# A gate-and-up projection with four K pairs as seven block products instead of three, and sums made by a DMA that adds

## The chip, the cores and the metric

The kernel runs on one core of one Trainium2 chip. The metric is the device time of one execution in microseconds (us). The profile was taken from one more execution, which has its own time.

## The reference

Two encoder layers over 256 tokens of 2048 features, all in float32. Each layer has a mixer (windowed attention, a convolution group and a gating group behind one input projection `w_in`, joined by `w_out`) and then a SwiGLU block, which is what the change touches:

```python
def swiglu(h, w_gate, w_up, w_down):
    return (jax.nn.silu(h @ w_gate) * (h @ w_up)) @ w_down

h = rms_norm(x, ffn_norm_g[l])
x = x + swiglu(h, w_gate[l], w_up[l], w_down[l])
```

`h` is 256 x 2048, `w_gate` and `w_up` are 2048 x 5632, `w_down` is 5632 x 2048.

## The kernel before

**Float32 from three products.** TensorE (PE) multiplies in a shortened format. So each weight tile is split into a high part `wh` (a cast on ScalarE, ACT, L136) and a low part `wl` (the rest, a subtraction on VectorE, DVE, L137), each activation tile likewise, and every product is three matmuls (`three_tok`, L410 to L412): high by high, low by high, high by low.

**Weights.** The host packs all weights into chunks of 128 x 2048, in the order of use. `Weights.load` brings a chunk into one of three `raw` buffers, by a DMA on SyncE's queue (SP, L94). `Weights.split` cuts it into units of at most 1024 columns and fills one of five pairs of `wh` and `wl` buffers. When the last unit of a chunk is split, the next chunk is asked for. `take` runs the splitting four units ahead of PE.

**Gate and up.** `gate_up` makes 512 columns of gate and of up for all 256 tokens. It is called 22 times, 11 for each layer. K is 2048, 16 tiles of 128, taken as eight pairs in the order of `UP_PAIRS`. The two token tiles and the two halves (gate, up) of a pair's weights make a 2 x 2 by 2 x 2 block product. A pair of kind "P" does it with eight products in two units. A pair of kind "S" does it in the Winograd way, with seven products in four units: two that come straight from the raw chunk (1024 and 512 columns) and two that are sums of weights. The first sum `f` has 1024 columns, one DVE addition (L101); the second, `g`, two DVE additions of 512 columns from `f` and raw columns. The sums of activations are made once for a layer (`feed_sums`). `f` and `g` lie in tiles with the tags `hm6` and `hm7`, which the mixer uses before.

**Results.** The products run into seven PSUM banks, m1 to m7. After the last S pair of a call (`LAST_S`) banks 1, 6 and 7 are read (L472 to L474), after the last pair the others (L476 to L480). Then silu and the multiplication (L828, L829). The tile is transposed during the next call (`hidden_parts`). After two or three calls a down projection follows (`ad` tiles).

**What sets the order.** A scheduler with a model of its own orders the instructions of each engine when the kernel is built; the tile pools give a buffer to a new tile when the last reader of the old one is done. Each engine and each DMA queue works its list in order.

The lines that matter: `UP_PAIRS` (L50), `Weights.load` (L87), `source` (L103), `split` (L125), `sum_tile` (L194), `gate_up` (L418).

Of the kernel before, what the change touches and what calls it, by code (L numbers as in the profile page):

```python
# [10 lines left out]
F32 = mybir.dt.float32  # L11
F32R = mybir.dt.float32r
AF = mybir.ActivationFunctionType
ALU = mybir.AluOpType
# [3 lines left out]
P = 128  # L18
D = 2048
S = 256  # L20
# [5 lines left out]
TAPS = 31  # L26
HALO = TAPS // 2
EPS = 1e-6
NU = 16
NEG = -3.0e38  # L30
SCALE = 1.0 / math.sqrt(128.0)
CH = 2048
HC = CH // 2
# [13 lines left out]
             (0, MIX_CONV, 1, 1, 1), (1, MIX_CONV, 1, 1, 1)]  # L47


UP_PAIRS = [(4, "P"), (5, "S"), (6, "P"), (7, "S"), (0, "P"), (1, "S"), (2, "P"), (3, "P")]  # L50
KIND = dict(UP_PAIRS)
LAST_S = max(i for i, (_, kind) in enumerate(UP_PAIRS) if kind == "S")

# [11 lines left out]
class Weights:  # L65
# [8 lines left out]
    def __init__(self, nc, w, kinds, raw_pool, split_pool, sum_tile):  # L74
        self.nc, self.w = nc, w
        self.n = w.shape[0]
        assert len(kinds) == self.n
        self.raw_pool, self.split_pool, self.sum_tile = raw_pool, split_pool, sum_tile
        self.units = [
            (i, u) for i in range(self.n) for u in range(4 if kinds[i] == "S" else 2)  # L80
        ]
        self.kinds = kinds
        self.raw, self.sums, self.parts = {}, {}, {}
        self.loaded = self.split_done = 0
        self.cur, self.off, self.width = -1, 0, 0

    def load(self, pieces=1, after_first=None):  # L87
        i = self.loaded
        if i >= self.n:
            return  # L90
        t = self.raw_pool.tile([P, CH], F32, tag="raw", name=f"raw{i}")
        for k in range(pieces):
            c = slice(k * CH // pieces, (k + 1) * CH // pieces)
            self.nc.sync.dma_start(t[:, c], self.w[i, :, c])  # L94
            if k == 0 and after_first:
                after_first()
        self.raw[i] = t
        self.loaded += 1

    def add(self, out, a, b):  # L100
# [2 lines left out]
    def source(self, i, u):  # L103
        raw = self.raw[i]
        if self.kinds[i] != "S":
            return raw[:, u * HC:(u + 1) * HC]
        if u == 0:
            return raw[:, HC:]
        if u == 1:
            return raw[:, 512:HC]  # L110
        if u == 2:
            f = self.sum_tile(0)
            self.add(
                f.rearrange("p (a b) -> p a b", a=2),
                raw[:, 0:512].unsqueeze(1).to_broadcast([P, 2, 512]),
                raw[:, 512:512 + HC].rearrange("p (a b) -> p a b", a=2),
            )
            self.sums[i] = f
            return f
        g = self.sum_tile(1)  # L120
        self.add(g[:, :512], self.sums.pop(i)[:, 512:], raw[:, 512:HC])
        self.add(g[:, 512:], g[:, :512], raw[:, HC + 512:])
        return g
# [36 lines left out]
def chunk_kinds():  # L160
    kinds = []
    for _ in range(DEPTH):
        kinds += ["P"] * (MIX_COLS * KT // CH + D * KT // CH)
        for _, gn in PARTS:
            kinds += [kind for _, kind in UP_PAIRS] * gn
            kinds += ["P"] * (4 * gn * D // CH)
# [4 lines left out]
def encoder_kernel(  # L171
# [15 lines left out]
    hpool = ctx.enter_context(tc.tile_pool(name="hpool", bufs=1))  # L187
    units = ctx.enter_context(tc.tile_pool(name="units", bufs=NU))
    tmp = ctx.enter_context(tc.tile_pool(name="tmp", bufs=2))
# [2 lines left out]
    pm = ctx.enter_context(tc.tile_pool(name="pm", bufs=2, space=PSUM))  # L192

    def sum_tile(i):  # L194
        return hpool.tile([P, HC], F32, tag=f"hm{6 + i}", name=f"fs{i}")

    W = Weights(nc, w, chunk_kinds(), raw_pool, split_pool, sum_tile)

    def unit(name, dtype=F32):
# [23 lines left out]
    hm = []  # L223
# [194 lines left out]
    def gate_up(forms, pending):  # L418
# [7 lines left out]
        plan = []  # L426
        for i, kind in UP_PAIRS:
            if kind == "S":
# [27 lines left out]
        for b, block in enumerate(plan):  # L456
            if b == 1 and pending:
                hidden_parts(*pending)
            if UP_PAIRS[b][1] == "S":
                for m, x, _ in block:  # L460
# [33 lines left out]
    def proj(kts, part, g):  # L494

        accs = [ps.tile([P, 512], F32, tag="ps", name=f"acc{i}") for i in range(g)]
        for i, k in enumerate(kts):
            wh, wl = W.take(g * P)
            for j in range(g):
                c = slice(j * P, (j + 1) * P)  # L500
                three(accs[j][:, :S], wh[:, c], wl[:, c], part(k, 0), part(k, 1),
                      i == 0, i == len(kts) - 1)
        return accs
# [205 lines left out]
    for l in range(DEPTH):  # L709
# [22 lines left out]
        for c in range(2, 4):  # L732
            a = proj(range(KT), xs_part, 1)[0]
            g = proj(range(KT), xs_part, 1)[0]
# [17 lines left out]
        for g in range(2):  # L752
            a = proj(range(KT), xs_part, 1)[0]
# [9 lines left out]
        for p in range(4):  # L763
            qT = unit2("qT")
            for hh in range(2):
                a = proj(range(KT), xs_part, 1)[0]
# [49 lines left out]
        def hidden_parts(ht, i0):  # L816
            for i in range(0, 4, 2):
                pt = transposed(ht, i)
                d = hm[(i0 + i) // 2]
                hilo(d[:, :, :S], d[:, :, S:], pt)  # L820

        for g0, gn in PARTS:
# [13 lines left out]
            for n in range(NG):  # L836
                acc = token_acc("ad")
                f = slice(n * G, (n + 1) * G)
# [34 lines left out]
def _pack_weights(w_in, w_out, w_gate, w_up, w_down):  # L873
# [17 lines left out]
    for l in range(DEPTH):  # L891
# [18 lines left out]
        for g0, gn in PARTS:  # L910
            for j in range(g0, g0 + gn):
                c = slice(j * G, (j + 1) * G)
                gu = np.concatenate([w_gate[l][:, c], w_up[l][:, c]], axis=1)
                for i, kind in UP_PAIRS:
                    pair = (2 * i, 2 * i + 1)
# [74 lines left out]
```

## Time and profile before

| | us |
|---|---|
| median of 3 runs (2002.52 to 2003.04) | 2002.74 |
| the profiled execution | 2004.66 |
| its span in the trace | 2002.9 |
| PE busy | 1973.4 |
| DVE busy | 1561.3 |
| ACT busy | 1060.3 |
| POOL (GpSimd) busy | 28.2 |

The span runs from the first to the last instruction. A busy time is the union of an engine's instructions; matmuls overlap one another, so their pace is read from their starts. A name such as `wl<-fs,wh` says that a `wl` tile was written from an `fs` and a `wh` tile. The releaser of a wait is the instruction whose end ended it.

### The profile page before, as it was taken

The numbers are of one execution on the slowest core, as the hardware profiler recorded it, in microseconds if no ns is written. First come the engines' busy times: TensorE is split into PE (matmuls) and PEld (weight loads), VectorE is DVE, ScalarE is ACT, GpSimd is POOL, SyncE is SP. The second block draws the span as 40 slices with busy tenths as digits, with TensorE's granted clock in tenths as the row PEclk, the third lists the DMA queues.
The fourth block names the chain that finished last, engine by engine and source line by source line (L and its number), as shares of the span: only waits on it lengthen the run. The fifth ranks groups of instructions, "written<-read, shape, count | busy, mean of one in ns | idle before, by whom it ended". The sixth has DMA issues, their size and how long they took to land.

```text
span 2002.9 us, 25520 instructions
## 1 busy us (share of the span) xinstructions
PE 1973.4 (99%) x9998; PEld 1683.8 (84%) x9998; DVE 1561.3 (78%) x1986; ACT 1060.3 (53%) x1367; POOL 28.2 (1%) x50
## 2 busy tenths in 40 slices
PE   8999999999999999999999999999999999999998
PEld 8998887888888888888899888788888888888886
DVE  8997679866886688578679975798678857985785
ACT  6356556544554455445544565665445544554553
POOL 3000000000000000000000000000000000000000
PEclk9999999999999999999999999999999999999999
DMA  7554544565555455555545435355545555555553
GB/s 276 202 183 154 203 158 178 198 212 186 192 208 208 170 210 204 196 189 204 196 169 190 148 139 202 143 192 207 210 170 208 211 191 187 210 204 192 192 204 111
DMA packets 55993, 380.96 MB, mean 190 GB/s; under 512 B 6336, under 2 KB 8640, under 8 KB 10560
## 3 DMA queue, kind: packets, MB, share of 16 engines
q1 hardware_dynamic: 55872, 379.33, 52.3%
q8 instruction: 78, 1.28, 0.2%
q14 instruction: 43, 0.35, 0.1%
HBM read 377.21 MB, written 2.10 MB: 189 GB/s over the span
## 4 chain that ended last, share of the span: by engine, by line
PE 97%; ACT 1%; DVE 1%; DMA 0%; issue 0%; SPq 0%; POOLq 0%; DVEq 0%
PE m L410 15%; PE m L411 15%; PE m L412 15%; PE ad L411 8%; PE ad L412 8%; PE ad L410 8%; PE acc L394 4%; PE acc L395 4%; PE acc L396 4%; PE ao L410 3%; PE ao L412 3%; PE ao L411 3%; PE pt L294 1%; PE acct L514 1%; PE acct L515 1%; PE acct L516 1%
## 5 line engine op out<-in xcount | busy, mean ns | idle before, releaser
L136 ACT CAST wh<-raw 128x1024 fp32r<-128x1024 f32 (+1 forms) x706 | 700.4, 1009 | 695.2 <-PE ad L412 243.5
L137 DVE TENSOR_TENSOR wl<-raw,wh 128x1024 fp32r<-128x1024 f32 (+1 forms) x706 | 816.7, 1168 | 313.8 <-ACT wh L136 310.7
L411 PE MATMUL m<-wl,xs 128*128 128x512 f32 x858 | 336.0, 392 | 0.0
L412 PE MATMUL m<-wh,xs 128*128 128x512 f32 x858 | 333.8, 391 | 0.0
L410 PE MATMUL m<-wh,xs 128*128 128x512 f32 x858 | 310.8, 392 | 7.1 <-ACT xg L317 7.1
L411 PE MATMUL ad<-wl,h 128*128 128x512 f32 x704 | 274.5, 390 | 0.0
L410 PE MATMUL ad<-wh,h 128*128 128x512 f32 x704 | 274.3, 391 | 0.0
L412 PE MATMUL ad<-wh,h 128*128 128x512 f32 x704 | 272.1, 390 | 0.0
L136 ACT CAST wh<-fs 128x1024 fp32r<-128x1024 f32 x132 | 138.8, 1053 | 159.8 <-PE m L412 133.8
L394 PE MATMUL acc<-xs,wh 128*128 128x256 f32 x704 | 196.8, 287 | 8.1 <-ACT xs L283 8.1
L395 PE MATMUL acc<-xs,wh 128*128 128x256 f32 x704 | 200.7, 287 | 0.0
L396 PE MATMUL acc<-xs,wl 128*128 128x256 f32 x704 | 200.3, 287 | 0.0
L137 DVE TENSOR_TENSOR wl<-fs,wh 128x1024 fp32r<-128x1024 f32 x132 | 159.9, 1220 | 47.7 <-ACT wh L136 47.5
L410 PEld LDWEIGHTS m<-wh,xs 128*128 128x128 f32 x858 | 162.4, 189 | 40.3 <-ACT xg L317 7.5
L412 PEld LDWEIGHTS m<-wh,xs 128*128 128x128 f32 x858 | 162.3, 189 | 33.9
L411 PEld LDWEIGHTS m<-wl,xs 128*128 128x128 f32 x858 | 162.1, 189 | 33.8
L412 PEld LDWEIGHTS ad<-wh,h 128*128 128x128 f32 x704 | 132.2, 188 | 27.3
L410 PEld LDWEIGHTS ad<-wh,h 128*128 128x128 f32 x704 | 132.2, 188 | 27.1
L411 PEld LDWEIGHTS ad<-wl,h 128*128 128x128 f32 x704 | 132.2, 188 | 26.9
L394 PEld LDWEIGHTS acc<-xs,wh 128*128 128x128 f32 x704 | 134.4, 194 | 8.7 <-ACT xs L283 8.4
L395 PEld LDWEIGHTS acc<-xs,wh 128*128 128x128 f32 x704 | 136.8, 194 | 0.2
L396 PEld LDWEIGHTS acc<-xs,wl 128*128 128x128 f32 x704 | 136.5, 194 | 0.2
(180 smaller groups left out, 2636.0 us busy)
## 6 DMA issues: line engine op xcount, KB each, us to landing
raw<-w SPq DMA_DIRECT2D x349, 1024.0 KB, 4.8
x<-xT SPq DMA_DIRECT2D x16, 128.0 KB, 4.6
raw<-w SPq DMA_DIRECT2D x4, 512.0 KB, 7.0
lr<-lrow SPq DMA_DIRECT2D x2, 1024.0 KB, 4.9
xt<-xN SPq DMA_DIRECT2D x2, 1024.0 KB, 6.0
raw<-w SPq DMA_DIRECT2D x4, 256.0 KB, 4.3
gf<-lrow SPq DMA_DIRECT2D x1, 1024.0 KB, 6.6
out<-xt SPq DMA_DIRECT2D x2, 448.0 KB, 3.5
```

The lines of the kernel that those rows point to most:

```text
L136: self.nc.scalar.copy(out=h[:, c], in_=r[:, c])
L137: self.nc.vector.tensor_tensor(out=lo[:, c], in0=r[:, c], in1=h[:, c].bitcast(F32), op=ALU.subtract)
L294: nc.tensor.transpose(pt[:, i, t * P:(t + 1) * P], src[t][:, (i0 + i) * P:(i0 + i + 1) * P], ident,)
L394: nc.tensor.matmul(acc, wh, xh, start=first, stop=False)
L395: nc.tensor.matmul(acc, wh, xl, start=False, stop=False)
L396: nc.tensor.matmul(acc, wl, xh, start=False, stop=last)
L410: nc.tensor.matmul(a, xh, wh, start=first, stop=False)
L411: nc.tensor.matmul(a, xh, wl, start=False, stop=False)
L412: nc.tensor.matmul(a, xl, wh, start=False, stop=last)
L514: nc.tensor.matmul(a, xh, wh, start=(k == 0), stop=False)
L515: nc.tensor.matmul(a, xh, wl, start=False, stop=False)
L516: nc.tensor.matmul(a, xl, wh, start=False, stop=(k == KT - 1))
```

## The change

`UP_PAIRS` gets a fourth "S" and another order of kinds: P S S P S P S P in place of P S P S P S P P. So a call has 60 products, and its last S pair is the seventh of eight instead of the sixth. The host packs the weights by the same table.

`f` is no longer added on DVE. When a chunk of kind "S" is loaded, `load` also issues a DMA on SP that writes the chunk's first 512 columns twice into a sum tile, and a DMA on GpSimd's queue that adds columns 512 to 1535 to it, straight from the weights in memory. `f` alternates between two tiles, one with a tag of its own (`fs`) and `hm6`; `g` takes `hm7`. The pool of small tiles grows from 16 to 17.

```diff
--- before.py
+++ after.py
@@ -26,7 +26,7 @@
 TAPS = 31
 HALO = TAPS // 2
 EPS = 1e-6
-NU = 16
+NU = 17
 NEG = -3.0e38
 SCALE = 1.0 / math.sqrt(128.0)
 CH = 2048
@@ -47,7 +47,7 @@
              (0, MIX_CONV, 1, 1, 1), (1, MIX_CONV, 1, 1, 1)]
 
 
-UP_PAIRS = [(4, "P"), (5, "S"), (6, "P"), (7, "S"), (0, "P"), (1, "S"), (2, "P"), (3, "P")]
+UP_PAIRS = [(4, "P"), (5, "S"), (6, "S"), (7, "P"), (0, "S"), (1, "P"), (2, "S"), (3, "P")]
 KIND = dict(UP_PAIRS)
 LAST_S = max(i for i, (_, kind) in enumerate(UP_PAIRS) if kind == "S")
 
@@ -81,7 +81,7 @@
         ]
         self.kinds = kinds
         self.raw, self.sums, self.parts = {}, {}, {}
-        self.loaded = self.split_done = 0
+        self.loaded = self.split_done = self.n_sums = 0
         self.cur, self.off, self.width = -1, 0, 0
 
     def load(self, pieces=1, after_first=None):
@@ -95,6 +95,14 @@
             if k == 0 and after_first:
                 after_first()
         self.raw[i] = t
+        if self.kinds[i] == "S":
+
+            f = self.sum_tile(self.n_sums % 2)
+            self.n_sums += 1
+            w12 = self.w[i, :, 0:512].unsqueeze(1).to_broadcast([P, 2, 512])
+            self.nc.sync.dma_start(f.rearrange("p (a b) -> p a b", a=2), w12)
+            self.nc.gpsimd.dma_start(f, self.w[i, :, 512:512 + HC], accum_op=ALU.add)
+            self.sums[i] = f
         self.loaded += 1
 
     def add(self, out, a, b):
@@ -109,15 +117,8 @@
         if u == 1:
             return raw[:, 512:HC]
         if u == 2:
-            f = self.sum_tile(0)
-            self.add(
-                f.rearrange("p (a b) -> p a b", a=2),
-                raw[:, 0:512].unsqueeze(1).to_broadcast([P, 2, 512]),
-                raw[:, 512:512 + HC].rearrange("p (a b) -> p a b", a=2),
-            )
-            self.sums[i] = f
-            return f
-        g = self.sum_tile(1)
+            return self.sums[i]
+        g = self.sum_tile(2)
         self.add(g[:, :512], self.sums.pop(i)[:, 512:], raw[:, 512:HC])
         self.add(g[:, 512:], g[:, :512], raw[:, HC + 512:])
         return g
@@ -192,7 +193,8 @@
     pm = ctx.enter_context(tc.tile_pool(name="pm", bufs=2, space=PSUM))
 
     def sum_tile(i):
-        return hpool.tile([P, HC], F32, tag=f"hm{6 + i}", name=f"fs{i}")
+        tag = ("fs", "hm6", "hm7")[i]
+        return hpool.tile([P, HC], F32, tag=tag, name=f"fs{i}")
 
     W = Weights(nc, w, chunk_kinds(), raw_pool, split_pool, sum_tile)
```

The scheduler orders the new program anew. Two places follow, in a call of the first layer. In the names, `fs0`, `fs1` and `fs2` are the sum tiles by their number, `wl212` the low part of unit 212, `m5` bank 5.

VectorE at the end of a call, before: from the evacuation of bank 6 (L473) on.

```order
L473 TENSOR_TENSOR u2_4575<-m6_4569,s1_4574 128x512
L137 TENSOR_TENSOR wl199_4802<-raw87_4708,wh199_4801 128x1024
L137 TENSOR_TENSOR wl200_4817<-raw88_4758,wh200_4816 128x1024
L474 TENSOR_TENSOR u3_4576<-m7_4568,u2_4575 128x512
L101 TENSOR_TENSOR fs0_4910<-raw89_4786 128x1024
L137 TENSOR_TENSOR wl201_4833<-raw88_4758,wh201_4832 128x1024
L101 TENSOR_TENSOR fs1_4928<-fs0_4910,raw89_4786 128x512
L137 TENSOR_TENSOR wl202_4851<-raw89_4786,wh202_4850 128x1024
L101 TENSOR_TENSOR fs1_4928<-fs1_4928,raw89_4786 128x512
L476 TENSOR_TENSOR s1_4574<-m2_4570,s1_4574 128x512
L137 TENSOR_TENSOR wl203_4867<-raw89_4786,wh203_4866 128x512
L478 TENSOR_TENSOR s3_4882<-m5_4572,s3_4882 128x512
```

The same place now, up to the low part of the first S pair's sum in the next call (`wl212`, from `fs0_4854`).

```order
L475 TENSOR_TENSOR u2_4627<-m6_4621,s1_4626 128x512
L138 TENSOR_TENSOR wl209_4902<-raw88_4804,wh209_4901 128x1024
L138 TENSOR_TENSOR wl210_4917<-raw89_4852,wh210_4916 128x1024
L476 TENSOR_TENSOR u3_4628<-m7_4620,u2_4627 128x512
L138 TENSOR_TENSOR wl211_4933<-raw89_4852,wh211_4932 128x512
L478 TENSOR_TENSOR s1_4626<-m2_4622,s1_4626 128x512
L480 TENSOR_TENSOR s3_4948<-m5_4624,s3_4948 128x512
L309 TENSOR_TENSOR c22_4949<-m5_4624,u3_4628 128x512
L138 TENSOR_TENSOR wl212_4977<-fs0_4854,wh212_4976 128x1024
L309 TENSOR_TENSOR s3_4948<-s3_4948,u2_4627 128x512
L482 TENSOR_TENSOR u3_4628<-m4_4625,u3_4628 128x512
L831 SCALAR_TENSOR_TENSOR s3_4948<-s3_4948,c1_b0_3121,s1_4626 128x512
```

The addition of 1024 columns (`fs0_4910<-raw89`) is gone, and the additions to `g` stand earlier, outside these rows. The evacuations of all banks follow one another more closely.

VectorE further on, now: up to the first reader of the third S pair's sum `fs0_5001`, which lies in the same buffer as `fs0_4854`.

```order
L831 SCALAR_TENSOR_TENSOR c22_4949<-c22_4949,c1_b0_3121,u3_4628 128x512
L138 TENSOR_TENSOR wl213_4996<-fs2_4992,wh213_4995 128x1024
L138 TENSOR_TENSOR wl214_5031<-raw90_4883,wh214_5030 128x1024
L109 TENSOR_TENSOR fs2_5057<-fs1_4885,raw90_4883 128x512
L138 TENSOR_TENSOR wl215_5041<-raw90_4883,wh215_5040 128x512
L138 TENSOR_TENSOR wl216_5048<-fs1_4885,wh216_5047 128x1024
L109 TENSOR_TENSOR fs2_5057<-fs2_5057,raw90_4883 128x512
L255 TENSOR_TENSOR h0_3_0_4956<-pt_5016,h0_3_0_4956 128x2x256
L138 TENSOR_TENSOR wl217_5061<-fs2_5057,wh217_5060 128x1024
L138 TENSOR_TENSOR wl218_5073<-raw91_4905,wh218_5072 128x1024
L109 TENSOR_TENSOR fs2_5130<-fs0_5001,raw92_4999 128x512
```

`fs1_4885` and `raw90_4883` are freed by two neighbouring rows, and the copy into `fs0_5001` can start once `wl212` is made, thirteen rows ahead of its first reader.

SyncE's queue at the place where these chunks are loaded, before: loads alone.

```order
L94 DMA raw89_4786<-w 128x2048
L94 DMA raw90_4805<-w 128x2048
L94 DMA raw91_4836<-w 128x2048
L94 DMA raw92_4935<-w 128x2048
L94 DMA raw93_4977<-w 128x2048
L94 DMA raw94_5027<-w 128x2048
```

SyncE's queue there now (L103 is the copy of the first 512 columns).

```order
L94 DMA raw91_4905<-w 128x2048
L94 DMA raw92_4999<-w 128x2048
L103 DMA fs0_5001<-w 128x2x512
L103 DMA fs1_5088<-w 128x2x512
L94 DMA raw93_5064<-w 128x2048
L94 DMA raw94_5086<-w 128x2048
L94 DMA raw95_5137<-w 128x2048
L103 DMA fs0_5215<-w 128x2x512
L94 DMA raw96_5165<-w 128x2048
```

GpSimd's queue there now (L104 is the DMA that adds); before, nothing stood here.

```order
L104 DMA fs0_4854<-w 128x1024
L104 DMA fs1_4885<-w 128x1024
L104 DMA fs0_5001<-w 128x1024
L104 DMA fs1_5088<-w 128x1024
L104 DMA fs0_5215<-w 128x1024
```

Copies stand among the loads, in the order in which their buffers come free, and each L104 waits for its L103.

## Rows read from the trace of the kernel before

**Rows 1.** The page's head: the span, and each engine's busy time.

```profile
span 2002.9 us, 25520 instructions
PE 1973.4 (99%) x9998; PEld 1683.8 (84%) x9998; DVE 1561.3 (78%) x1986; ACT 1060.3 (53%) x1367; POOL 28.2 (1%) x50
```

**Rows 2.** Windows over two calls: us, each engine's busy time, PEclk, DMA share, GB/s.

```profile
711.02:753.55 42.53, 42.53 (x193) 35.15 (x192) 37.83 (x44) 24.41 (x29) 0.00 (x0) 1.00 0.55 198
753.55:796.08 42.53, 42.53 (x193) 35.21 (x192) 37.94 (x44) 24.51 (x29) 0.00 (x0) 1.00 0.54 198
```

**Rows 3.** Timeline of PE in a call: start, us, engine, line, operation.

```profile
716.68 0.39 PE L410 MATMUL m<-wh,gd 128*128 128x512 f32 x1
...
725.97 0.39 PE L412 MATMUL m<-wh,xs 128*128 128x512 f32 x1
...
728.24 0.39 PE L410 MATMUL m<-wh,gh 128*128 128x512 f32 x1
```

**Rows 4.** Groups of PE by line: count, busy us and mean ns, idle before.

```profile
L410 PE MATMUL m<-wh,xs 128*128 128x512 f32 x858 | 310.8, 392 | 7.1 <-ACT xg L317 7.1
...
L410 PE MATMUL m<-wh,gh 128*128 128x512 f32 x264 | 97.7, 400 | 0.0
L410 PE MATMUL m<-wh,gd 128*128 128x512 f32 x220 | 85.8, 390 | 0.0
```

**Rows 5.** Groups of DVE by line and shape: the sums of weights.

```profile
L101 DVE TENSOR_TENSOR fs<-fs,raw 128x512 f32<-128x512 f32 x132 | 90.5, 685 | 0.8
L101 DVE TENSOR_TENSOR fs<-raw 128x1024 f32<-128x1024 f32 x66 | 80.5, 1220 | 13.7 <-DMA raw<-w 13.2
```

**Rows 6.** Timeline of DVE at the end of a call.

```profile
711.62 2.35 DVE L137 TENSOR_TENSOR wl<-raw,wh 128x1024 fp32r<-128x1024 f32 x2
...
722.24 0.68 DVE L307 TENSOR_TENSOR s<-s,u 128x512 f32<-128x512 f32 x1
722.84 0.68 DVE L480 TENSOR_TENSOR u<-m,u 128x512 f32<-128x512 f32 x1
723.44 1.21 DVE L137 TENSOR_TENSOR wl<-fs,wh 128x1024 fp32r<-128x1024 f32 x1
724.57 0.74 DVE L829 SCALAR_TENSOR_TENSOR s<-s,c_b,s 128x512 f32<-128x512 f32 x1
725.23 0.74 DVE L829 SCALAR_TENSOR_TENSOR c<-c,c_b,u 128x512 f32<-128x512 f32 x1
...
728.67 1.23 DVE L137 TENSOR_TENSOR wl<-fs,wh 128x1024 fp32r<-128x1024 f32 x1 [1.57 <-ACT wh L136]
```

**Rows 7.** Timeline of ACT in the same call.

```profile
707.66 2.95 ACT L136 CAST wh<-raw 128x1024 fp32r<-128x1024 f32 x3
```

**Rows 8.** The page's DMA issues: KB each, median us to landing.

```profile
tb<-tab SPq DMA_DIRECT2D x1, 512.0 KB, 4.0
```

**Rows 9.** The raw loads on SP's queue: who waited for them, and landing.

```profile
L94 SPq DMA_DIRECT2D raw<-w x357: 327/328/432, 0.7 to 1967.4; - x179
...
  DVE fs L101: 13.2, 19
  ACT wh L136: 6.9, 6
...
DMA to landing us min/median/max: 3.4/4.8/8.5
```

**Rows 10.** DMA in the call from 711.02 to 753.55, in 40 slices and by queue.

```profile
GB/s 139 431 416 277 416 247 62 247 447 231 177 385 362 62 0 0 0 8 15 0 0 139 239 424 385 378 370 39 0 0 139 378 439 231 447 347 0 0 0 46
...
q1 hardware_dynamic: 1152, 8.39, 54.6%
```

**Rows 11.** Groups of POOL by line.

```profile
L275 POOL TENSOR_TENSOR sqacc_in<-sqacc_in,sq 128x256 f32<-128x256 f32 x14 | 13.1, 937 | 13.4 <-ACT sq L271 12.5
L373 POOL TENSOR_TENSOR c_a<-c_a,misc 128x2 f32<-128x2 f32 x2 | 3.4, 1724 | 699.2 <-DVE c_a L369 699.2
```

**Rows 12.** DVE on the tile xs from 0 to 40 us: ns min/median/max.

```profile
L284 DVE SCALAR_TENSOR_TENSOR xs<-x,cs,xs x16: 473/956/964, 5.4 to 28.2; 128x256 fp32r<-128x256 f32 x16
```

## Prediction

> **What bounds the kernel now.** I began with the page's summary [rows 1]: TensorE (PE) is busy for 1973.4 of 2002.9 us, VectorE (DVE) for 1561.3, ScalarE (ACT) for 1060.3, GpSimd (POOL) for 28.2. That share alone does not say that PE sets the pace inside the gate-and-up stage, so I cut out two neighbouring calls of `gate_up`, from one L473 to the next [rows 2]. In each, 42.53 us long, PE has no idle time at the full clock (PEclk 1.00), DVE works 37.8 to 37.9 us and ACT 24.4 to 24.5 us, and the DMA engines are busy for 0.54 to 0.55. DVE has under 5 us to spare in a call. Then the pace of a matmul. A PE row lasts 0.39 us, but rows overlap; starts count. From 716.68 to 725.97 us there are 41 steps [rows 3], so 9.29 / 41 = 0.2266 us each. A call has 61 products of three matmuls, 183 of them: the three groups that start a product count 858 + 264 + 220 = 1342 [rows 4], which is 22 calls of 61. 183 x 0.2266 = 41.47 us; eight transposes and 0.2 to 0.3 us of small gaps fill the 42.53.
>
> So in this stage a matmul that goes is worth its step, as long as DVE, ACT and the loads still deliver each unit in time.
>
> **What is removed on PE.** One pair per call changes from eight products to seven: three matmuls, in 22 calls 66. 66 x 0.2266 = 14.96 us. Nothing lies beside them that would hold the end up in their place, so all of it counts if no new wait comes up. A call would take 42.53 - 0.68 = 41.85 us.
>
> **What happens on DVE.** Per call, three f additions go (1024 columns), one S pair more brings one 1024-column and one 512-column split beyond the two splits that the P pair had, and two 512-column g additions. The additions last 1.22 and 0.685 us [rows 5], but DVE starts its next instruction before one ends: two 1024-column splits take 2.35 us together, so that the second adds 1.13, and 512-column evacuations start 0.60 us apart, at 722.24 and 722.84 [rows 6]. Sum: -3 x 1.13 + 1.13 + 0.60 + 2 x 0.60 = -0.46 us. From 37.9 us it goes to 37.4 of 41.85: the spare time is 4.4 us where it was 4.6. ACT gains a 1024-column cast at 0.95 (three take 2.95 us [rows 7]) and a short one, some 1.5 us, and has 17 us free; that is hidden.
>
> The last S block is now the seventh, with one P block behind it instead of two. The evacuation of banks 6 and 7 (L473, L474) and that of banks 2, 3, 5 and 4 fall within one P block, 24 steps or 5.4 us. The order of DVE, below the diff in the document, shows what stands there: from L475 to the last reader of bank 5, L309, there are two long splits, a short one and five evacuations, 2 x 1.13 + 6 x 0.60 = 5.9 us. PE needs bank 5 not at the head of the next call but later, since the program puts the first products into that bank behind those of the next S pair, as it did before. With DVE on time this costs nothing. If it is late there, PE pays the lateness; I keep 0 to 0.5 us per call, 0 to 11 us, and take 0.
>
> **What the two new DMAs cost.** This is the unknown: the trace of before has no DMA on POOL and none that adds. First the room, then the price.
>
> The room in time is tightest for the third S pair of a call. Its copy into fs0 may start only after the first S pair's sum has been split (in the order fence, `wl212<-fs0`), because both use one buffer; its first reader is the addition `fs2<-fs0` with thirteen DVE instructions between: six of 0.60, two of 0.66 (L829 starts at 724.57 and 725.23) and five splits of 1.13 [rows 6], 10.6 us of work. DVE also waits for ACT there, which waits for PE to release a buffer; such a wait before a split is 1.57 us at 728.67 [rows 6]. And PE works some units behind DVE: the split that starts at 723.44 [rows 6] is done at 724.65, and PE's first product with a sum comes at 728.24 [rows 3], 3.6 us later. I count half of that as reserve at the tighter place, an estimate. Room, then: 10.6 + 1.6 + 1.8 = 14 us.
>
> The copy is 512 KB; the nearest row is 4.0 us for 512 KB (tb) [rows 8]. The addition is at least such a transfer, 4.0 us, behind what POOL needs to start it: between nothing and 1.72 us, the mean of its two-element operations, and I take 1, near the 0.94 of its most frequent one [rows 11]. For an addition that reads two sources I take the landing of a 1024 KB load, 4.8 us [rows 9]. Sum 4.0 + 1 + 4.8 = 9.8 us; ends 8.0 and 4.0 + 1.7 + 8.5 (the longest landing of a raw load [rows 9]) = 14.2 us. The middle leaves 4 us; the upper end leaves none.
>
> The room in bandwidth: a call loads 8.39 MB with 54.6% of 42.53 us [rows 10], 23.2 us, so 512 KB cost 1.45 us of all 16 engines. The four copies cost 5.8 us. Four additions cost 5.8 us if each is like a plain copy (lower end), 11.6 us if it is like two (weights and old sum are read), 17.4 if like three. I take two. Together 34.8, 40.6 or 46.4 us per call. 41.85 us are there, so the middle would fill the engines to 97%. But these prices come from a stretch in which the queue runs dry again and again; where it is full, the same row of slices shows up to 447 GB/s [rows 10], and 8.39 + 2.1 + 4.2 MB at that rate are 33 us. So between 33 and 41 us: it fits, without much air. By row, a load is asked for when its buffer comes free, and DVE and ACT waited for a load only 13.2 and 6.9 us in the whole run [rows 9]; I take no stall from that.
>
> [...]
>
> **The queues.** On SP the copies stand among the loads [order fence]; each waits for a sum buffer, and the raw loads behind it wait too. In the rows shown the buffer's last reader stands just ahead of the reader that frees the next raw buffer, so a load starts under 1.2 us later; with 19 and 6 waits for loads in 357 [rows 9] most have that to spare. On POOL an addition waits for its copy, and behind it stand the other additions and the small L373 and L651 operations; L373's result in a layer's first call is needed only at the call's end. Both cost nothing.
>
> **Sum.** 2002.9 - 14.96 = 1987.9 us of span; the profiled execution took 2004.66 us, 1.8 us more than its span, so 1989.7. It lay 1.9 us above the median of 2002.74; against that the forecast is 2002.74 - 14.96 = 1987.8, rounded to 1988.
>
> **Rivals.**
>
> 1. The additions fill the DMA engines (slower). The place is the whole gate-and-up stage; it decides from the point where one addition costs more than (41.85 - 23.2 - 5.8) / 4 = 3.2 us of all engines, that is 2.2 plain copies. At three copies a call takes 46.4 us, 3.9 more than now, and 22 calls make 85 us: 2088. At 2.5 copies 43.5 us, and 2024. For it: that my middle already fills 97% by the mean price. Against: 447 GB/s in slices. I count the late sum with it: a chain of 16 us, 2 over the room, stalls PE 2 us per call, 44 us in all, and gives 2032. Together 0.26.
>
> 2. POOL and DVE get in each other's way. At the start POOL adds squares in 0.94 us each [rows 11], and DVE's L284 beside them takes 0.956 us at the median and 0.473 at the least [rows 12]: a DVE operation beside a busy POOL can last 0.48 us longer. If each of four additions holds DVE up for 0.5 to 1 us, DVE's 37.4 us become 39.4 to 41.4 of 41.85, and the gain is half lost or lost: 1995 to 2003. [...] 0.14 together with the case that DVE is late at the end of a call.
>
> [...]
>
> **Chances.** Forecast 0.60 (1988, its own range 1986 to 1996 with partial losses). Rival 1 0.26, 2010 to 2088. Rival 2 0.14, mostly 1995 to 2003. A change of 0.2%, 4 us, is what a measurement of this kernel tells from none. Faster: all of the forecast and a little of rival 2, 0.62. Same: 0.11. Slower: 0.27. The range goes from 1985 to 2040: below, PE cannot give more than its 66 steps and a few tenths of us per call; above, it takes in half of rival 1.
>
> **What would show it.** Right: L410 to L412 on m count 66 fewer in all; the span between two L475 is near 41.85 us with PE without idle; the additions land within 6 us; DMA share in a call is 0.75 to 0.95. Wrong: PE waits for `wh<-fs` or `wl<-fs` behind a DMA; DMA share at 1.0 in a call; DVE's 1024-column operations longer than 1.22 us; or additions that take over 10 us to land.

## The result and the profile after

The changed kernel takes 2107.09 us (median of 4 runs, 2102.45 to 2110.11), the kernel before 2002.89 beside it: a ratio of 1.0517 with a 95% interval of 1.0503 to 1.053. It is 104 us slower; 1988 was forecast, and the range ended at 2040. The page's head, which answers to [rows 1]:

```profile
span 2100.7 us, 25999 instructions
...
PE 1998.8 (95%) x9932; PEld 1674.1 (80%) x9932; DVE 1546.7 (74%) x2014; ACT 1088.3 (52%) x1411; POOL 109.6 (5%) x138
```

PE has its 66 matmuls less (9932 for 9998) and is yet busy for longer: at 2100.7 us of span it stands idle for 102 us where it stood for 29.5. DVE and ACT work as long as forecast and less of the span. So something waits. Two neighbouring calls, as in [rows 2], each from one L475 to the next:

```profile
752.08:798.47 46.39, 45.02 (x202) 36.66 (x200) 36.67 (x43) 26.43 (x32) 2.62 (x3) 1.00 0.88 277
798.47:842.56 44.09, 39.34 (x167) 30.07 (x167) 36.66 (x44) 23.66 (x28) 3.48 (x4) 1.00 0.87 266
```

These calls take 44 to 46 us instead of 42.53, at the full clock (1.00), with PE idle for up to 4.75 us of them; the DMA engines are busy for 0.87 to 0.88, not full. Taken from the first to the last matmul on `m`, the eight gate-and-up stages of the run last 1042.7 us in all, where they lasted 943.7 before; these 99 us are the whole difference of the spans, 97.8 us. One stage of three calls, before and now:

```profile
679.96:806.52 126.56, 126.56 (x567) 104.73 (x566) 108.50 (x118) 72.31 (x81) 0.00 (x0) 1.00 0.55 199
705.98:847.51 141.53, 130.09 (x559) 104.08 (x558) 107.19 (x121) 75.83 (x86) 9.59 (x11) 0.98 0.82 257
```

A part of the loss is PE's clock. In this stage PE stood for 5.3 us behind a late sum, and after it the granted clock was 0.50 of full speed:

```profile
731.00:736.00 5.00, 1.21 (x6) 0.67 (x4) 1.05 (x2) 1.01 (x1) 0.00 (x0) 0.93 0.88 307
736.00:742.00 6.00, 4.48 (x11) 3.51 (x12) 5.48 (x6) 0.70 (x2) 0.86 (x1) 0.50 0.55 109
```

From 738.11 to 741.95 us the matmuls start 0.427 us apart, where the step is 0.227 at the full clock. Over the whole run the granted clock is 0.987, where it was 0.997 before. By this it costs at most 0.010 x 2100.7 = 21 of the 98 us, an estimate that takes PE as busy all the time. The lower clock goes with the waits: with three sum tiles, below, the granted clock is 0.999.

The engines' shares of the chain that ended last, and below them the waits by engine (us in all, times, longest):

```profile
PE 56%; DMA 24%; DVE 13%; issue 4%; ACT 2%; DVEq 0%; SPq 0%; POOLq 0%; ACTq 0%
```

```profile
DVE fs L109 <- DMA fs<-w: 119.8, 26, 6.7
ACT wh L137 <- DMA raw<-w: 85.4, 53, 3.9
ACT wh L137 <- DVE fs L109: 83.8, 45, 3.2
PEld m L413 <- DVE wl L138: 79.7, 44, 5.7
ACT wh L137 <- DMA fs<-w: 74.3, 26, 4.8
```

PE alone does not set the end any more. Read from the bottom up: ACT and DVE wait for a sum that a DMA writes, and PE waits for DVE's split. Before, no such wait was there, and casts waited for a raw load for 6.9 us in all [rows 9]. The DMA part of the page says why the sums are late (queues; then issues with KB each and median us to landing):

```profile
q0 software_dynamic: 12672, 46.14, 12.4%
...
raw<-w SPq DMA_DIRECT2D x349, 1024.0 KB, 5.6
fs<-w SPq DMA_DIRECT2D x88, 512.0 KB, 7.9
fs<-w POOLq DMA_DIRECT2D x88, 512.0 KB, 8.8
```

The copy lands in 7.9 us (forecast 4.0, from [rows 8]) and the addition in 8.8 (forecast 4.8, from [rows 9], behind 1 us for POOL). The 5.6 us of the raw loads is a median of the whole run. In the stage of three calls alone they land in 7.7 us, and in the same stage before in 4.8:

```profile
raw<-w SPq DMA_DIRECT2D x24, 1024.0 KB, 4.8
raw<-w SPq DMA_DIRECT2D x23, 1024.0 KB, 7.7
```

So everything that is transferred in the stage lands late, the copies in 7.5 us and the additions in 8.7 at the median. The additions' share of the engines, on the other hand, is as forecast: 12.4% of 2100.7 us over 88 additions is 2.96 us each, against 2.9.

At the place that the prediction called tightest, the third S pair of a call, the chain that ended last reads (start us, us, what):

```profile
805.01 1.14 DVE wl L138
806.16 0.02 issue
806.17 6.86 DMA fs<-w
...
813.11 0.60 issue
813.70 4.81 DMA fs<-w
818.51 4.57 issue
823.08 0.69 DVE fs L109
```

The split that ends at 806.15 is the last reader of the sum tile; the copy starts at once and lands after 6.9 us, POOL issues the addition at 813.7, and DVE can add to the sum at 823.08 only, 9.4 us later: 16.9 us from the tile's release to its next sum. Of the addition's time 4.57 us are put down as "issue": for them the profile shows nothing that DVE waited for. DVE's own timeline shows how much of these 16.9 us was room:

```profile
804.94 1.21 DVE L138 TENSOR_TENSOR wl<-fs,wh 128x1024 fp32r<-128x1024 f32 x1
...
817.28 1.22 DVE L138 TENSOR_TENSOR wl<-raw,wh 128x1024 fp32r<-128x1024 f32 x1
823.08 0.69 DVE L109 TENSOR_TENSOR fs<-fs,raw 128x512 f32<-128x512 f32 x1 [4.58 <-issue]
```

From 806.15 to 818.50 it had work or short waits, 12.3 us; then it stood for 4.58 us.

This is one of the longer chains at this place: over the 22 calls the third S pair's takes 11.9 to 17.9 us, 12.9 at the median. Worse off is the fourth S pair, with 18.1 us at the median. In the two calls before this one VectorE waited there as follows:

```profile
734.91 1.42 DVE L109 TENSOR_TENSOR fs<-fs,raw 128x512 f32<-128x512 f32 x2 [6.52 <-DMA fs<-w]
784.25 0.69 DVE L109 TENSOR_TENSOR fs<-fs,raw 128x512 f32<-128x512 f32 x1 [4.50 <-DMA fs<-w]
```

Summed over all calls, VectorE waits before its first L109 of an S pair for 47.1 us at the first S pair (mostly for a raw load), 0.7 at the second, 47.0 at the third and 92.4 at the fourth.

### The profile page after: what moved, and what is told of

It is laid out like the page before. It is cut to its first block, busy times and chain, and to the rows that moved or that the text cites. A ratio compares the mean times of both kernels' runs of the same rounds, so it can differ in the third digit from the quotient of the medians.

```text
span 2100.7 us, 25999 instructions
## 1 busy us (share of the span) xinstructions
PE 1998.8 (95%) x9932; PEld 1674.1 (80%) x9932; DVE 1546.7 (74%) x2014; ACT 1088.3 (52%) x1411; POOL 109.6 (5%) x138
## 3 DMA queue, kind: packets, MB, share of 16 engines
q0 software_dynamic: 12672, 46.14, 12.4%
## 4 chain that ended last, share of the span: by engine, by line
PE 56%; DMA 24%; DVE 13%; issue 4%; ACT 2%; DVEq 0%; SPq 0%; POOLq 0%; ACTq 0%
DMA fs<-w 19%; DVE wl L138 8%; PE ad L412 8%; PE ad L413 8%; PE ad L414 8%; DMA raw<-w 5%; PE acc L396 4%; PE acc L397 4%; PE acc L398 4%; PE m L413 4%; PE m L414 3%; PE m L412 3%; DVE fs L109 3%; PE ao L412 2%; PE ao L414 2%
## 5 line engine op out<-in xcount | busy, mean ns | idle before, releaser
L138 DVE TENSOR_TENSOR wl<-raw,wh 128x1024 fp32r<-128x1024 f32 (+1 forms) x706 | 803.4, 1151 | 284.0 <-ACT wh L137 281.5
L137 ACT CAST wh<-raw 128x1024 fp32r<-128x1024 f32 (+1 forms) x706 | 687.5, 994 | 614.6 <-PE ad L414 216.6
L413 PE MATMUL m<-wl,xs 128*128 128x512 f32 x792 | 318.0, 401 | 60.3 <-DVE wl L138 60.2
L414 PE MATMUL m<-wh,xs 128*128 128x512 f32 x792 | 313.2, 397 | 0.0
L137 ACT CAST wh<-fs 128x1024 fp32r<-128x1024 f32 x176 | 184.7, 1049 | 232.0 <-DVE fs L109 83.5
L412 PE MATMUL m<-wh,xs 128*128 128x512 f32 x792 | 280.2, 398 | 4.0 <-ACT wh L137 2.6
L109 DVE TENSOR_TENSOR fs<-fs,raw 128x512 f32<-128x512 f32 x176 | 121.0, 687 | 187.9 <-DMA fs<-w 119.8
L138 DVE TENSOR_TENSOR wl<-fs,wh 128x1024 fp32r<-128x1024 f32 x176 | 211.5, 1219 | 31.9 <-ACT wh L137 31.9
L412 PEld LDWEIGHTS m<-wh,xs 128*128 128x128 f32 x792 | 150.4, 191 | 44.3 <-ACT wh L137 11.1
L414 PEld LDWEIGHTS m<-wh,xs 128*128 128x128 f32 x792 | 152.2, 192 | 31.3
L104 POOL DMA_DIRECT2D fs<-w x88 | 76.9, 874 | 1469.2 <-DMA fs<-w 612.4
L413 PE MATMUL m<-wl,gh 128*128 128x512 f32 x352 | 139.0, 395 | 2.2 <-DVE wl L138 1.5
```

Source lines behind the costliest of these rows:

```text
L104: self.nc.gpsimd.dma_start(f, self.w[i, :, 512:512 + HC], accum_op=ALU.add)
L109: self.nc.vector.tensor_tensor(out=out, in0=a, in1=b, op=ALU.add)
L137: self.nc.scalar.copy(out=h[:, c], in_=r[:, c])
L138: self.nc.vector.tensor_tensor(out=lo[:, c], in0=r[:, c], in1=h[:, c].bitcast(F32), op=ALU.subtract)
L412: nc.tensor.matmul(a, xh, wh, start=first, stop=False)
L413: nc.tensor.matmul(a, xh, wl, start=False, stop=False)
```

## The experiments

Theory A, after the result: the chain copy, addition, sum is longer than the room, because two tiles hold four sums a call; PE waits for it. Two rivals: the additions fill the DMA engines, so that raw loads come late; or the new order with its fourth S pair asks too much of ACT and DVE.

**Four sum tiles.** Two more tiles of 4 KB are lent by rows that the mixer and the final norm need; those rows are then loaded in two halves.

```diff
-            f = self.sum_tile(self.n_sums % 2)
+            f = self.sum_tile((0, 1, 3, 4)[self.n_sums % 4])
```

> The sums of the S pairs rotate among four tiles instead of two (two 4 KB tiles that hold mixer and final-norm rows are lent during the gate-and-up stage), so that a copy no longer waits for the sum of the S pair two back. Theory A, the late chain: copy 6.9 and addition 9.3 us start only when the old sum is split, and DVE and PE wait for them; with the buffer free long before, the waits of DVE and ACT for a sum (119.8 + 74.3 us) go and the time falls to 1988 to 1996 us. Theory B, full DMA engines: 38.2 us of transfers in a call of 44.1 leave no room whenever they start; the time stays at 2085 to 2110 us, with longer landings.

Measured: 2006.81 us, ratio 1.002 [1.0008, 1.0032]. 100 of the 104 us are gone with the same bytes, the same order and as many additions, so A holds for them, and full DMA engines were not the cause. But the time lies above A's range, too: the 15 us of the removed matmuls don't appear. What still waits in this run:

```profile
ACT wh L137 <- DMA raw<-w: 78.2, 47, 4.7
ACT wh L137 <- DVE fs L109: 52.6, 29, 3.1
DVE fs L109 <- DMA raw<-w: 50.4, 29, 3.6
PEld m L416 <- ACT wh L137: 18.6, 29, 1.4
DVE fs L109 <- DMA fs<-w: 11.8, 3, 4.2
```

The wait for the addition has shrunk from 119.8 to 11.8 us; now PE waits for casts, in small pieces.

**Sums on DVE.** Four S pairs in the changed order, the sums formed as before; the two DMAs go from `load`.

```diff
-            return self.sums[i]
+            f = self.sum_tile(0)
+            self.add(f..., raw[:, 0:512]..., raw[:, 512:512 + HC]...)
```

> The fourth S pair and the new order of kinds alone: the first sums are added on VectorE as before, no copy and no adding DMA. Theory A and theory B both say that the stall comes with the DMAs, so PE saves its 66 matmuls, 15 us, unless VectorE is now too loaded: per call it carries 1.13 + 4 x 1.13 - 3 x 1.13 + 1.8 = 4.1 us more than before, 42.0 of 41.85 us. I expect 1995 to 2015 us. A theory C, that the order of kinds itself makes PE wait at the end of a call, expects 2040 us or more.

Measured: 2006.33 us, 1.0015 [1.0006, 1.0025]. That is within the expected range, and far below theory C's 2040. It is as slow as four tiles, without any of the new DMAs. What eats the gain in these two runs is common to them: the order P S S P S P S P, or the fourth S pair. Without the DMAs the raw loads are not what is late; casts wait for VectorE's sums:

```profile
ACT wh L136 <- DVE fs L101: 68.0, 34, 3.1
ACT wh L136 <- DMA raw<-w: 5.6, 6, 1.9
```

**Three S pairs in the old order**, with sums by DMA.

```diff
-UP_PAIRS = [(4, "P"), (5, "S"), (6, "S"), (7, "P"), (0, "S"), (1, "P"), (2, "S"), (3, "P")]
+UP_PAIRS = [(4, "P"), (5, "S"), (6, "P"), (7, "S"), (0, "P"), (1, "S"), (2, "P"), (3, "P")]
```

> The DMA sums alone: the old kinds P S P S P S P P with three S pairs, their first sums by copy and adding DMA. Three sums per call load the DMA engines with 23.2 + 3 x 1.56 + 3 x 2.96 = 36.8 us of 42.53. Theory A: the buffer of a sum is free again two S pairs later, 4 chunks or some 21 us, which is more than the 16 us of the chain; no stall, 2000 to 2006 us. Theory B: 87% of the engines are asked for, as now, and the loads come late; 2040 to 2090 us.

Measured: 2007.24 us, 1.0017 [1.0007, 1.0026]. That is 1 us above A's range and far below B's. DVE's busy time falls to 1487.3 us and nothing comes of it; PE did not wait for DVE before. Two tiles are enough for three sums a call: VectorE's additions wait for raw loads, 38.4 us in all, and not for a sum.

**A second DMA that overwrites instead of adding** (it leaves the first 512 columns out of the sums).

```diff
-            self.nc.gpsimd.dma_start(f, self.w[i, :, 512:512 + HC], accum_op=ALU.add)
+            self.nc.gpsimd.dma_start(f, self.w[i, :, 512:512 + HC])
```

> The changed kernel with the second DMA as a plain copy on GpSimd's queue that overwrites instead of adding (the first 512 columns are left out of the sums). Everything else, the waits included, stays. Measures what the adding costs: an addition lands 8.8 us after its issue, and takes 2.96 us of all engines. Theory A: it lands after 4 to 5 us like other 512 KB transfers, the chain is 4 us shorter, and the time falls to 2000 to 2030 us. Theory B: the engines are relieved by 1.5 us for each of four, 6 us per call, and the time falls as far, but the landings of raw loads fall too, from 7.7 us in a call to near 5.

Measured: 2031.91 us, 1.0144 [1.0129, 1.0159]. Its DMA rows, to be read against those of the changed kernel:

```profile
q0 software_dynamic: 12672, 46.14, 7.1%
...
fs<-w SPq DMA_DIRECT2D x88, 512.0 KB, 7.0
fs<-w POOLq DMA_DIRECT2D x88, 512.0 KB, 5.9
```

The same bytes without the addition land in 5.9 us instead of 8.8 and take 7.1% x 2028.3 / 88 = 1.64 us of the engines instead of 2.96, 1.8 times less. The chain is 3.8 us shorter by these medians, and 75 of the 104 us go, to 2 us above A's range. Raw loads in a stage of three calls land in 6.8 us instead of the changed kernel's 7.7, not near 5 as B said. VectorE still waits 78.3 us for sums, nearly all of it at the fourth S pair of a call.

**The two S pairs drawn apart, and shorter raw loads.** The first run draws the two S pairs apart with the two tiles of the change. The others leave the unused first 512 columns out of the S pairs' raw loads (the DMAs read them from memory): with four tiles in the changed order, then with the pairs drawn apart and two tiles, then with the pairs drawn apart and four.

```diff
-UP_PAIRS = [(4, "P"), (5, "S"), (6, "S"), (7, "P"), (0, "S"), (1, "P"), (2, "S"), (3, "P")]
+UP_PAIRS = [(4, "S"), (5, "P"), (6, "S"), (7, "P"), (0, "S"), (1, "P"), (2, "S"), (3, "P")]
...
+        lo = 512 if self.kinds[i] == "S" else 0
-            c = slice(k * CH // pieces, (k + 1) * CH // pieces)
+            c = slice(max(lo, k * CH // pieces), (k + 1) * CH // pieces)
```

> The changed kernel with its two sum tiles, the four S pairs placed in alternation (S P S P S P S P instead of P S S P S P S P). Every sum tile now has four chunks, some 20 us of PE, from one use to the next, where the third S pair of a call had three. Theory A, the late chain of 16.7 us (copy 7.9, addition 8.8): it fits in 20 us, and most of the 104 us go; 1990 to 2015 us. Theory B, full DMA engines: the bytes are the same, the time stays above 2080 us. For the 15 us that were missing with four sum tiles and with sums on VectorE: theory O, the order (two S pairs in a row, and VectorE late at the end of the call) expects them back here, 1988 to 1996 us; theory R, raw loads that come late between the other transfers, expects 2003 to 2015.

Measured: 2137.48 us, 1.0667 [1.0642, 1.0692]. My expectation failed: a more even order gave the chain no more room. The time is one that theory B allowed, but the runs with more tiles below move the same bytes and are fast. The chain that ended last in this run shows what I had overlooked:

```profile
738.34 0.70 DVE fs L109
...
739.67 5.24 DVE wl L138 x5
...
744.93 8.26 DMA fs<-w
...
753.86 5.78 DMA fs<-w
...
764.34 0.10 DVE fs L109
```

It is a ring. VectorE first uses a tile's sum at 738.34 and splits it, the tile is released and copied into at 744.93, added to at 753.86, and its next sum is used at 764.34: a turn of 26.0 us. The same tile's next turns take 23.8 and 25.0 us. Each of two tiles is turned twice in a call, and a call cannot be shorter than two turns, wherever the pairs stand. The stage of three calls has 147.2 us here, six turns of 24.5 if all were alike, and 141.5 in the changed kernel, six of 23.6; single turns in that stage take from 19.9 to 29.4 us. At the other tile VectorE waits in most turns for a raw load that comes late.

> Four sum tiles, the order of the change, and the raw load of an S chunk without its first 512 columns, which nothing reads since the copy fetches them from memory itself: 1.0 MB per call less, 2.9 us of all engines. Theory R, late raw loads (ACT waited for them 78 us, VectorE's additions 50 us with four sum tiles): these waits fall to less than half and the time from 2006.8 to 1990 to 1998 us. Theory O, the order: the waits fall, but the time stays at 2001 to 2007 us.

Measured: 1996.61 us, 0.9958 [0.9945, 0.9971], 0.6% below four tiles with whole loads; casts wait for raw loads for 35.1 us instead of 78.2, VectorE's additions for 31.0 instead of 50.4. The time is theory R's, and not theory O's: in this order with four tiles, late raw loads cost some 10 us.

> Alternating S pairs with two sum tiles, and raw loads of S chunks without the first 512 columns. Theory O: no better than the alternation alone by more than 3 us, 1987 to 1995. Theory R: 5 to 12 us better than the alternation alone.

Measured: 2118.37 us, 1.0587 [1.0561, 1.0612]. That is 19 us below the alternation alone, more than either theory gave, but far above both ranges, which had counted on the alternation: the ring stays.

> Alternating S pairs, four sum tiles, short raw loads: every wait that the theories name is taken away, and PE should be left with its own steps, 2002.9 - 15.0 = 1988 us, give or take 3. If it stays above 1997, both theories miss what holds PE.

Measured: 1984.28 us, 0.9903 [0.9889, 0.9918]: faster than both kernels, and 0.7 us below the expected 1985 to 1991.

**A copy of rows that lie together.** It leaves W1 out of the second half of the sums.

```diff
-            w12 = self.w[i, :, 0:512].unsqueeze(1).to_broadcast([P, 2, 512])
-            self.nc.sync.dma_start(f.rearrange("p (a b) -> p a b", a=2), w12)
+            w12 = self.w[i, :, 0:HC]
+            self.nc.sync.dma_start(f, w12)
```

> As the changed kernel (two sum tiles, pairs P S S P S P S P), but the copy reads 4 KB that lie together, W1 and W2's first half, instead of the same 2 KB of W1 twice: this leaves W1 out of the second half of the sums. Theory A, the turn of a tile: two tiles are each filled twice in a call, and a call lasts two turns; a turn in the changed kernel is 139.5 / 6 = 23.3 us, of which the copy's landing is 7.9. A1, the copy is slow because it shares the DMA engines with raw loads and the other addition: it still lands in over 7 us, the stage of three calls still lasts 136 to 142 us, and the time stays at 1.04 to 1.055. A2, the copy is slow because it reads 2 KB rows twice: it lands like a raw load, 5.0 to 5.6 us, the turn falls to about 20.8 us, a call to 41.6, the stage to 125 to 129 us, the time to 2005 to 2025 us.

Measured: 2082.36 us, 1.0393 [1.0359, 1.0427]; the copy lands in 6.9 us, 1.0 less. Between the two expectations, much nearer to A1: the form of the copy is worth about 25 of the 104 us, and most of its landing is not its form. A2's 5.0 to 5.6 us were whole-run medians of raw loads; in a stage of this run the raw loads land in 7.3 us and the copies in 6.8.

**Which part of the fast version does it.** The first run has the pairs drawn apart, four tiles and whole raw loads; the second goes from four tiles to three by this edit.

```diff
-            f = self.sum_tile((0, 1, 3, 4)[self.n_sums % 4])
+            f = self.sum_tile((0, 1, 3)[self.n_sums % 3])
```

> Pairs in the order S P S P S P S P and four sum tiles, raw loads whole. It tells apart what brought the 1984.28 us of the version that also has short raw loads. Turn theory: with four tiles a call needs one turn of 24 us, so no wait for a sum is left, and the two S pairs that stand side by side in the changed kernel's order are gone: 1983 to 1990 us, no wait of the matmuls of m. Load theory: four whole raw loads instead of three quarters of each bring 1.0 MB more in a call, as they cost the other order 10 us (2006.81 against 1996.61): 1991 to 1999 us, with casts that wait for raw loads for over 60 us in all.

Measured: 1986.73 us, 0.9918 [0.9901, 0.9934]. The order alone took four tiles from 2006.81 to here, and the short loads add nothing that the intervals tell apart; the load theory falls for this order (casts wait 37.4 us for raw loads, where it asked for over 60).

> As the run with pairs S P S P S P S P and four sum tiles, but three tiles in turn. Turn theory: each tile is filled 4/3 times in a call, which needs 1.33 x 24 = 32 us of the call's 40.9: no wait for a sum, and a time within 0.3% of the run with four tiles. Rival, a tile must be free long before its copy is due, because copies and additions queue behind one another: three tiles lie between two (2137) and four, at 2000 to 2060 us, with VectorE waiting for the addition for over 40 us in all.

Measured: 1985.09 us, 0.9911 [0.9896, 0.9926], the same as with four. This is the number that the ring gives and a queue of DMAs behind one another does not: 4/3 of a turn fits into a call, two turns don't. Its head, a stage of three calls, and its DMA rows:

```profile
span 1983.1 us, 26010 instructions
...
PE 1956.6 (99%) x9932; PEld 1665.9 (84%) x9932; DVE 1545.4 (78%) x2014; ACT 1093.0 (55%) x1411; POOL 110.4 (6%) x139
```

```profile
671.68:796.45 124.77, 124.77 (x559) 103.18 (x558) 107.61 (x121) 76.47 (x86) 10.32 (x12) 1.00 0.91 289
```

```profile
fs<-w SPq DMA_DIRECT2D x88, 512.0 KB, 9.4
fs<-w POOLq DMA_DIRECT2D x88, 512.0 KB, 9.1
```

A call takes 124.77 / 3 = 41.6 us. PE has no idle time in the stage, though copy and addition land later than in the changed kernel and the engines are busier, 0.91 against 0.82. Landings of 9.4 and 9.1 us cost PE nothing here, with a third tile in turn.

Another rival is the queue on SP, where a copy that waits for its tile holds up the raw loads behind it. It does not account for the time: the copies wait as long in this run as with two tiles and the same order, 2137.48 us. The waits of SP for a split before a copy, with two tiles and with three:

```profile
SPq L103 <- DVE wl L138: 90.9, 79, 3.3
SPq L103 <- DVE wl L138: 89.8, 77, 3.3
```

**The order with sums on DVE**, without the DMAs, in one tile for `f` and one for `g`:

> Pairs in the order S P S P S P S P, the f sums formed by VectorE in two tiles, no copy and no addition by DMA. It asks whether the DMAs are needed for the gain of the version with three tiles (1985.09 us). Order theory: what cost 20 us in the run with VectorE's sums (2006.33) and in that with four tiles (2006.81) are the two S pairs side by side, whose casts and splits must come in one run; in turn with P pairs VectorE's 82% is enough and the time is 1983 to 1992 us. Rival, VectorE has too little to spare: each call adds four f additions of 1.13 us as pipelined, 4.5 us, to 35.9 of 40.7 us, which is 40.4 of 40.7; PE waits for the casts of sums as before, 1998 to 2012 us.

Measured: 1990.1 us, 0.9933 [0.9916, 0.995]. Its edit is the order of the fifth run upon that of the second.

```profile
PE 1960.4 (99%) x9932; PEld 1669.1 (84%) x9932; DVE 1639.5 (82%) x2102; ACT 1097.1 (55%) x1411; POOL 32.1 (2%) x50
```

The order theory holds: from 2006.33 to 1990.1 by the order of the pairs alone, with DVE at 82%. Most of the gain that the fourth S pair has to give needs no DMA; the DMAs, given a third tile, are worth some 5 us more at the medians, and the two intervals overlap.

## Why the prediction was wrong

**PE: right in size.** 66 matmuls less were priced at 14.96 us. Where next to nothing waits (three tiles, pairs in turn) the span falls by 19.8 us. Over the eight stages PE's busy time falls there from 936.7 to 921.5 us, by 15.2, close to that price. Its idle time in them falls from 7.1 to 4.0 us, and 1.6 us go outside them. The 7.1 us were a wait of matmuls on `m` for ACT's `xg` [rows 4], which in that run is 1.6 us:

```profile
L416 PE MATMUL m<-wh,xs 128*128 128x512 f32 x792 | 278.5, 390 | 1.6 <-ACT xg L323 1.6
```

Why that wait shrinks was not tried.

**The failed step: the price of the chain against its room.** The prediction set 14 us of room against 4.0 + 1 + 4.8 = 9.8 us, and counted this as 4 us to spare. The room on VectorE, priced at 10.6 + 1.6 = 12.2 us, came out at 12.3; the 1.8 us that PE works behind VectorE were an estimate that no run measured. The chain shown above was 16.9 (12.9 at the median of the 22 calls): the copy 6.9 instead of 4.0, the addition, from POOL's issue to its sum, 9.4 instead of 1 + 4.8, with 0.7 us between them. POOL's own part of that, priced at 1 us, was 0.87. (The 1.72 us at the upper end is the mean of one group of POOL's two-element operations, [rows 11]; the others are shorter.)

Both landings were priced from rows of a quieter queue: one tb load [rows 8] and raw loads at a DMA share of 0.55 [rows 2]; here the share is 0.87 in the calls shown. The 4.0 us of tb was a single load, and the lowest of its kind: in the thirteen other runs the same load landed in 4.4 to 7.8 us. The page of before also had four loads of 512 KB that landed late:

```profile
raw<-w SPq DMA_DIRECT2D x4, 512.0 KB, 7.0
```

With 7.0 us for the copy and for the addition the same sum would have been 15 us, more than the room. By the overwriting second DMA 2.9 us of an addition's landing are the adding itself; I had taken the landing of a load of twice the size as the measure for that, 0.8 us over tb's. The upper end that I kept, 14.2 us, was too low too: I let only the addition land late, and not the copy.

The place was wrong as well. I took the third S pair as the tightest and worked out no room for the fourth, where VectorE waited 92.4 us in all, twice as long as at the third.

**The second error, within rival 1.** "A chain of 16 us, 2 over the room, stalls PE 2 us per call, 44 us in all, and gives 2032." That chain is nearly what came, but a late sum does not stall once in a call. Its tile is released late as well, so the next copy starts late, and both tiles pay. VectorE waits at the third and at the fourth S pair, (47.0 + 92.4) / 22 = 6.3 us a call; the calls of the changed kernel are (141.53 - 124.77) / 3 = 5.6 us longer than those of the run with three tiles. So rival 1's mechanism came, in its half of the late sum, at more than twice its price.

**The engines' time: right.** 2.96 us per addition against 2.9; the engines were not full, and the limit of 3.2 us was not reached. The run with three tiles moves the same bytes in 41.6 us a call. A resource at 87% was not the bound. Landings on which a chain hung were longer at the higher load (raw loads 4.8 us at 0.55, 7.7 at 0.82 in the changed kernel's stage); that the load alone makes them longer was not isolated by a run.

**DVE: right in busy time, and rival 2 fell.** Its busy time falls by 14.6 us from [rows 1], where 22 x 0.46 = 10.1 of pipelined time was forecast. Beside the additions a split takes as long as ever:

```profile
L138 DVE TENSOR_TENSOR wl<-fs,wh 128x1024 fp32r<-128x1024 f32 x176 | 211.5, 1219 | 31.9 <-ACT wh L137 31.9
```

1219 ns against 1.21 and 1.23 us in [rows 6]. On POOL's side the issue of an addition took 862 to 1037 ns in 88 additions, 874 at the mean, with DVE busy for 74% of the span. That an addition costs the engines two plain copies was my choice between three prices; beside the overwriting transfer it was 2.96 against 1.64 us, 1.8 times. That is a rate, and the time was lost by a landing.

**A step that was missing: the order.** I costed the fourth S pair by sums over a call and looked at the call's end. That two S pairs now stand side by side got no sentence from me. With four tiles it costs 2006.81 - 1986.73, 20 us, with sums on DVE 16 us: by itself it would have turned my forecast of -15 into no change. What is late there is not one thing. With four tiles, short raw loads bring 10 of the 20 us back without a change of order, so about half of them are late loads, for which the prediction took no stall. With sums on DVE casts wait 5.6 us for loads and 68.0 for sums, and 16 us are lost all the same.

## What to carry to other kernels

When a buffer is filled by a chain that starts at its own release, count the turn of the ring (hold, copy, addition, landing) and multiply by turns per iteration and buffer; where they came out above the iteration's length, every iteration paid (two tiles: 47.2 us a call in the stage shown). Where the turns fit (three tiles: 41.6 us) they cost nothing here. But the sum is not enough where the uses stand unevenly: each use needs its own room, and I had worked it out for one of four. Price a landing from transfers at the load that will be there, not at the load of before (here raw loads of 4.8 us at a DMA share of 0.55 became 7.7 at 0.82); busy shares told here that the bytes fit, and not when they arrived, and a median over the whole run (5.6 us) hid how late they landed in one stage (7.7). And when a change brings a new order with it, test the order alone: here it was worth as much as the whole gain.

## What the hardware showed that I had not expected

- A DMA of 512 KB that adds to what lies in SBUF took 2.96 us of 16 engines and landed in 8.8 us; the same bytes as an overwrite took 1.64 and landed in 5.9.
- In a stage of the changed kernel a load of 1024 KB landed in 7.7 us and a copy of 512 KB in 7.5 (medians): half the bytes came hardly sooner. Reading 4 KB that lie together instead of 2 KB twice took 1.0 us off the copy's median over the run; the rest is open.
- The DMA engines at 0.91 busy held up no matmul in the stage shown, while at 0.82 in the changed kernel's stage transfers stood on the path, for 24% of that run's chain.
